# A two-layer block on one core: one rotation table, split modulation loads, paired squares, a shorter 1/rms and a divided FFN buffer

## The chip, the cores and the metric

The kernel runs on one core of one Trainium2 chip. The metric is the device time of one execution in microseconds (us). The core has five engines that run their own instruction streams and wait for each other through semaphores: TensorE (PE, matmul, with its weight loads PEld), VectorE (DVE), ScalarE (ACT), GpSimd (POOL) and SyncE (SP), which here issues the weight loads.

## The reference

Two transformer layers stand one behind the other, on 512 tokens of 1024 features, all in float32. What is computed, in short:

```python
# first layer
sh1, sc1, gt1, sh2, sc2, gt2 = adaln_params(c, w_mod, b_mod)     # silu(c) @ w_mod + b_mod
px = project(modulate(x, norm1_g, sh1, sc1), w_in)               # the same for ctx, 256 tokens
og = gla_bidir(...)                                              # gated linear attention, two directions
od = diff_attend(rope(rms(q)), rope(rms(k)) with ctx keys, v)    # differential attention
x = x + gt1 * (concat(merge(og), merge(od)) @ w_out)
x = x + gt2 * swiglu(modulate(x, norm2_g, sh2, sc2), w_ffn_in, w_ffn_out)
# second layer
h = rms_norm(x, mix_pre_g) @ w_in                                # pooling, forgetting attention, gates
x = x + rms_norm(mix, mix_post_g)
x = x + rms_norm(mem_attention(rms_norm(x), rms_norm(mem)))      # 256 memory tokens
x = x + rms_norm(conv_ffn(rms_norm(x), w_up, conv_w, w_down))    # hidden width 2816
```

Every norm divides by a root of a mean square over the 1024 features (or over a head). The modulation vectors come from a product of a 2-row matrix (c and c_ctx) with 1024 x 6144 weights.

## The kernel before, in words

**Layout and precision.** Activations stand feature-major, as eight tiles of 128 features by 512 tokens. A float32 product is made of three fast products: each operand is split in a high and a low part (`hi`, `lo`), and hi.hi, lo.hi and hi.lo are summed in PSUM. `wsplit` (L171) loads a weight piece of 512 KB to a ring buffer `wf` (two buffers), casts it on ACT to `whi` (L185), and subtracts on DVE or POOL to `wlo` (L186). `mm3` (L194 to L196) issues the three matmuls. So each weight piece costs one load, one ACT cast, one DVE subtraction and its matmuls.

**Start.** `normed_x` (L424) squares the eight tiles of x, by turns on ACT and DVE, and `sum_sq` (L308) sums each over features by four small matmuls with a vector of ones. `warm` (L483) issues spare transposes of an identity: 12 ahead of the first sum, two ahead of each later one (WU, WX). `rms` (L150 to L169) turns the sum into r = 1/rms by a logarithm and an exponential on ACT and a correction step on DVE; `bcast` (L326) spreads r over partitions by matmuls against the identity (L329), and ACT copies it out (L330). The first modulation tiles (`mod_tiles`, L350) come by 1 MB loads; ACT copies the sum (`mr`), two transposes (L362) bring it to columns, and DVE reduces it (L363).

**The first layer's middle.** Sixteen units of the linear attention (chunk, head) run in order from about 190 to 310 us. Projections, modulation steps and later work are "fillers": a list of closures with a length each, of which `fill_in` runs as many as fit between two parts of a unit. A modulation step (`mod_step`, L750 to L768) loads 512 KB of `w_mod` to the same ring `wf` as the weights and issues four matmuls (L762) into a PSUM bank; after four steps ACT copies 128 x 512 out (L766), and `mod_end` transposes it by four matmuls (L362). Twenty-four steps stand in units 0 to 11, two in each; eight stand in the filler list between `mem_in` and `mem_k`. The table of rotations is loaded once to `cs64`; GpSimd multiplies it by the key gain into `csk` and by the query gain in place (L630 to L635).

**Second norm of the first layer.** The output projection gives x in two halves of 256 tokens; `norm2` (L1299) computes sums (L311), r_n and its broadcast for each half, with pauses (`yield`) in which other matmuls are issued; W4 says how many stand ahead of the sums.

**FFN.** `ffn_hidden` (L1330) keeps the hidden activations as `Fhi` and `Flo`, and while these are empty uses parts of them as room for split weights (L1339, L1340). The second layer's FFN opens its pool `fp2` when the last residual update, `X<-X,KV` (L1428), is still running; the pool lies where `KV` and `Ym`, the halves of the branch just added, lay.

**Order.** The kernel names instructions behind which others are issued (`issue_after`, `queued`), and each engine executes its own list strictly in the order of the built program. SP's list holds nearly all loads, so a load that waits for its buffer holds back all loads behind it.

## Time and profile before

| | us |
|---|---|
| median of three runs | 1653.22 |
| lowest, highest | 1652.99, 1656.14 |
| the profiled execution's own time | 1654.39 |
| its span in the trace | 1652.6 |
| PE busy | 1600.5 (97%) |
| PE weight loads busy | 1359.2 (82%) |
| DVE busy | 948.7 (57%) |
| ACT busy | 716.8 (43%) |
| POOL busy | 214.1 (13%) |

The page lists the busy time of each engine over the whole span; the views quoted below list single instructions in order of time, who waited for whom, and the busy time of engines in short stretches with the clock that TensorE was granted (1.00 is 2.4 GHz, 0.50 is 1.2 GHz). In a row of a timeline the bracket at the end is the time for which the engine stood idle ahead of the instruction and who released it.

### The profile page before, as it was taken

The numbers are of one execution on the slowest core, as the hardware profiler recorded it, in microseconds if no ns is written. First come the engines' busy times: TensorE is split into PE (matmuls) and PEld (weight loads), VectorE is DVE, ScalarE is ACT, GpSimd is POOL, SyncE is SP. The second block draws the span as 40 slices with busy tenths as digits, with TensorE's granted clock in tenths as the row PEclk, the third lists the DMA queues.
The fourth block names the chain that finished last, engine by engine and source line by source line (L and its number), as shares of the span: only waits on it lengthen the run. The fifth ranks groups of instructions, "written<-read, shape, count | busy, mean of one in ns | idle before, by whom it ended". The sixth has DMA issues, their size and how long they took to land.

```text
span 1652.6 us, 25497 instructions
## 1 busy us (share of the span) xinstructions
PE 1600.5 (97%) x10146; PEld 1359.2 (82%) x10146; DVE 948.7 (57%) x1799; ACT 716.8 (43%) x1345; POOL 214.1 (13%) x236
## 2 busy tenths in 40 slices
PE   8998999999999999999999999999998999999997
PEld 6898877768999888888889777888988988888887
DVE  5647787868756222223335676445788777776333
ACT  3534445567745323232223565224466544444221
POOL 0400000111012222110004000122000222221001
PEclk9999999999999999999999999999999999999998
DMA  9132245232323333332332212234210223323332
GB/s 373 53 95 81 79 152 160 80 122 74 130 72 109 90 91 101 102 91 89 101 117 71 77 39 64 90 102 146 86 50 27 90 90 102 102 90 96 96 93 74
DMA packets 48903, 162.98 MB, mean 99 GB/s; under 512 B 5648, under 2 KB 11280, under 8 KB 47248
## 3 DMA queue, kind: packets, MB, share of 16 engines
q1 hardware_dynamic: 45040, 157.74, 30.5%
q10 hardware_dynamic: 3456, 3.33, 0.7%
q8 instruction: 80, 1.31, 0.3%
q0 software_dynamic: 288, 0.28, 0.1%
q14 instruction: 39, 0.32, 0.1%
HBM read 158.46 MB, written 3.15 MB: 98 GB/s over the span
## 4 chain that ended last, share of the span: by engine, by line
PE 87%; DVE 6%; ACT 3%; issue 2%; DMA 1%; POOL 1%; ACTq 0%; DVEq 0%; POOLq 0%
PE acc L194 16%; PE acc L195 16%; PE acc L196 16%; PE s L195 5%; PE s L196 5%; PE s L194 5%; PE acc L284 3%; PE acc L283 2%; PE acc L285 2%; PE mis L1135 2%; PE mis L1607 1%; PE acc L762 1%; DVE wlo L186 1%; DMA wm<-in_w_mod 1%; PE s L1106 1%
## 5 line engine op out<-in xcount | busy, mean ns | idle before, releaser
L185 ACT CAST whi<-wf 128x1024 fp32r<-128x1024 f32 (+4 forms) x221 | 228.7, 1035 | 421.1 <-PE acc L195 291.0
L186 DVE TENSOR_TENSOR wlo<-wf,whi 128x1024 fp32r<-128x1024 f32 (+2 forms) x183 | 221.7, 1211 | 176.2 <-ACT whi L185 170.8
L195 PE MATMUL acc<-qlo,whi 128*128 128x512 f32 (+1 forms) x640 | 238.9, 373 | 0.0
L196 PE MATMUL acc<-qhi,wlo 128*128 128x512 f32 (+1 forms) x640 | 238.9, 374 | 0.0
L194 PE MATMUL acc<-qhi,whi 128*128 128x512 f32 (+1 forms) x640 | 238.6, 373 | 0.0
L194 PEld LDWEIGHTS acc<-qhi,whi 128*128 128x128 f32 x640 | 120.7, 189 | 19.7
L195 PEld LDWEIGHTS acc<-qlo,whi 128*128 128x128 f32 x640 | 120.6, 189 | 19.6 <-issue 0.2
L196 PEld LDWEIGHTS acc<-qhi,wlo 128*128 128x128 f32 x640 | 120.7, 189 | 19.4
L195 PE MATMUL s<-qlo,whi 128*128 128x512 f32 (+1 forms) x336 | 127.4, 379 | 0.0
L194 PE MATMUL s<-qhi,whi 128*128 128x512 f32 (+1 forms) x336 | 127.4, 379 | 0.0
L196 PE MATMUL s<-qhi,wlo 128*128 128x512 f32 (+1 forms) x336 | 127.4, 379 | 0.0
L186 POOL TENSOR_TENSOR wlo<-wf,whi 128x1024 fp32r<-128x1024 f32 x38 | 90.9, 2393 | 213.5 <-ACT whi L185 213.5
L1392 DVE TENSOR_TENSOR e<-e,s 128x512 f32<-128x512 f32 (+1 forms) x22 | 14.3, 652 | 154.0 <-PE s L196 153.8
L195 PE MATMUL acc<-glo,whi 128*128 128x512 f32 (+1 forms) x208 | 74.5, 358 | 0.1
L196 PE MATMUL acc<-ghi,wlo 128*128 128x512 f32 (+1 forms) x208 | 74.2, 357 | 0.0
L194 PE MATMUL acc<-ghi,whi 128*128 128x512 f32 (+1 forms) x208 | 74.2, 357 | 0.0
L194 PEld LDWEIGHTS s<-qhi,whi 128*128 128x128 f32 x336 | 63.2, 188 | 11.9
L196 PEld LDWEIGHTS s<-qhi,wlo 128*128 128x128 f32 x336 | 63.2, 188 | 11.9
L195 PEld LDWEIGHTS s<-qlo,whi 128*128 128x128 f32 x336 | 63.2, 188 | 11.6
L194 PE MATMUL acc<-Fhi,whi 128*128 128x512 f32 (+1 forms) x187 | 71.5, 383 | 0.0
L196 PE MATMUL acc<-Fhi,wlo 128*128 128x512 f32 (+1 forms) x187 | 71.5, 383 | 0.0
L195 PE MATMUL acc<-Flo,whi 128*128 128x512 f32 (+1 forms) x187 | 71.5, 382 | 0.0
(648 smaller groups left out, 3832.0 us busy)
## 6 DMA issues: line engine op xcount, KB each, us to landing
wf<-in_w_ffn_in SPq DMA_DIRECT2D x44, 512.0 KB, 3.6
wf<-in_w_up SPq DMA_DIRECT2D x44, 512.0 KB, 3.5
wm<-in_w_mod SPq DMA_DIRECT2D x32, 512.0 KB, 4.1
wm<-in_w_mod SPq DMA_DIRECT2D x8, 1024.0 KB, 13.1
wf<-in_w_ffn_out SPq DMA_DIRECT2D x16, 512.0 KB, 3.6
wf<-in_w_g SPq DMA_DIRECT2D x16, 512.0 KB, 3.5
wf<-in_w_down SPq DMA_DIRECT2D x16, 512.0 KB, 3.5
wf<-in_w_dv SPq DMA_DIRECT2D x8, 512.0 KB, 4.2
```

Of the source, the lines that this page charges most:

```text
L185: A.copy(hi[:, :n], wf[:, :n])
L186: (lo_eng or V).tensor_tensor(lo[:, :n], wf[:, :n], f32(hi[:, :n]), ALU.subtract)
L194: T.matmul(o, lhi, rhi, start=start, stop=False)
L195: T.matmul(o, lhi, rlo, start=False, stop=False)
L196: ins = T.matmul(o, llo, rhi, start=False, stop=stop).ins
L283: T.matmul(o, bhi(k), whi, start=k == 0, stop=False)
L284: T.matmul(o, bhi(k), wlo, start=False, stop=False)
L285: T.matmul(o, blo(k), whi, start=False, stop=k == KT - 1)
L762: T.matmul(p[32 * j:32 * j + 32, 256 * h:256 * h + 256], silc[:, 4 * kc + j], wf[:, j * 256:(j + 1) * 256], start=kc == 0, stop=kc == 1, s ...
L1106: T.matmul(s_[:, n0:n1], QF[:, c, ts], KA[:, c, n0:n1], start=True, stop=False)
L1135: T.matmul(p[:, :128], aT[:, kt * 128:(kt + 1) * 128], v, start=kt == 0, stop=kt == NKT - 1)
L1607: T.matmul(pO[:, ts], vz[:, kt, hp_, 64 * e:64 * e + 128], pT[:, kt * 128:(kt + 1) * 128], start=kt + e == 0, stop=kt - t + e == 1, skip_g ...
```

## The change

Eight edits, none of which alters what is computed:

1. Start: squares in pairs. ACT squares tile k, DVE squares tile k+1 and adds the two; `sum_sq` runs four times instead of eight. The DVE square has one buffer. WU goes from 12 to 15, WX from 2 to 1. The first modulation tiles are queued behind the last sum, and the broadcast of r is cut in two around the transposes. The load of `cols` goes from ACT's queue to SP's.
2. `rms`: the logarithm reads the sum in PSUM with scale and bias, DVE forms v beside it, and three DVE operations follow where there were four.
3. The first loads of `memT` on ACT's queue are issued behind a later instruction (`hi_at`).
4. One rotation table: `csk` goes; `cs64` is turned for the keys, loaded again behind the w_dv loads, and turned for the queries (`turn_q`).
5. Modulation: of each two steps the first loads to a buffer of its own, the second to the ring; a group is two steps and 256 columns instead of four and 512, so ACT copies and `mod_end` come after every unit. The eight late steps go in groups of two behind two gate jobs and the first two `mem_k` jobs, and `mem_k` comes directly behind `mem_in`.
6. Second norm: the residual updates of the three finished parts come ahead of their squares; W4 goes from 2 to 1, and for the second half three pauses instead of one stand between sums and broadcast.
7. `ffn_hidden`: `Fhi` is cut in `Fhi` (7 tiles) and `Fend` (4 tiles, allocated first), rooms are taken from tiles 0 to 5 in order, and `zl` is allocated at its first use.
8. The ring's buffer count gets a name (NWF, 2 as before).

```diff
-WU, WX, WW = 12, 2, 5
+WU, WX, WW = 15, 1, 5
-W4, W5 = 2, 1
+W4, W5 = 1, 1
...
+        A.activation(y, src, AF.Ln, scale=scale, bias=epsc)
         V.tensor_scalar(v, src, scale, EPS, ALU.mult, ALU.add)
-        A.activation(y, v, AF.Ln)
         last_rs[0] = A.activation(y, y, AF.Exp, scale=-0.5).ins
-        V.tensor_tensor(t, y, y, ALU.mult)
-        V.tensor_tensor(t, t, v, ALU.mult)
-        V.tensor_scalar(t, t, -0.5, 1.5, ALU.mult, ALU.add)
-        V.tensor_tensor(r, y, t, ALU.mult)
+        V.scalar_tensor_tensor(t, v, -0.5, y, ALU.mult, ALU.mult)
+        V.tensor_tensor(t, t, y, ALU.mult)
+        V.scalar_tensor_tensor(r, t, 1.5, y, ALU.add, ALU.mult)
...
-        nc.scalar.dma_start(cols, a["cols"])
+        nc.sync.dma_start(cols, a["cols"])
...
-            for k in range(KT):
-                t = st2.tile([128, S], F32, tag=f"sqt{k % 2}", name="sqt")
-                if k % 2:
-                    V.tensor_tensor(t, x[:, k], x[:, k], ALU.mult)
-                else:
-                    A.activation(t, x[:, k], AF.Square)
+            for k in range(0, KT, 2):
+                t, u = (st2.tile([128, S], F32, tag=f"sqt{j}", name="sqt", bufs=2 - j) for j in range(2))
+                A.activation(t, x[:, k], AF.Square)
+                V.tensor_tensor(u, x[:, k + 1], x[:, k + 1], ALU.mult)
+                V.tensor_tensor(u, u, t, ALU.add)
                 with tc.issue_after(warm(WU if k == 0 else WX)):
-                    sum_sq(pt, t, k == 0, k == KT - 1)
+                    last_warm[0] = sum_sq(pt, u, k == 0, k == KT - 2)
...
-        mod_tiles(8)
-        next(nx)
-        im = mod_tiles(0)
+        queued(last_warm[0], lambda: mod_tiles(8))
+        ins = next(nx)
+        im = queued(ins, lambda: mod_tiles(0))
+        with tc.issue_after(ins):
+            next(nx)
...
+    def turn_q():
+        nc.sync.dma_start(cs64, a["rope"])
+        turn("q_g")
+    turn("k_g")
...
+        if (w, hf) == ("w_dv", 0) and len(fillers) == 12:
+            fillers.append((0.0, turn_q))
...
-        nc.scalar.dma_start(m, a["memT"][:, k])
+        with tc.issue_after(hi_at[0]):
+            nc.scalar.dma_start(m, a["memT"][:, k])
...
-        wf = ring.tile([128, RW], F32, tag="wf", name="wm", bufs=2)[:, :1024]
+        wf = ring.tile([128, RW], F32, tag="wf", name="wm", bufs=NWF)[:, :1024] if kc else \
+            mid2.tile([128, 1024], F32, tag="wm", name="wm", bufs=1)
...
-        if h == 1 and kc == 1:
-            mr = mid2.tile([128, 512], F32, tag="mr", name="mr")
-            A.copy(mr, p)
+        if kc == 1:
+            mr = mid2.tile([128, 256], F32, tag="mr", name="mr")
+            A.copy(mr, p[:, :256])
...
-        if u % 2 == 0:
-            mod_end()
+        mod_end()
...
+    mods_left = [[(0.8, mod_step), (0.8, mod_step), (0.3, mod_end)] for _ in range(MU, 16)]
     for m in range(GR, 4):
         fillers.append(gr_jobs[m])
+        fillers += mods_here()
...
-    for n in range(MU // 2, 8):
-        fillers += [(0.8, mod_step) for _ in range(4)] + [(0.6, mod_end)]
     for m in range(4):
         fillers.append((1.45, lambda m=m: mem_k(m)))
+        fillers += mods_here()
...
         r = fm_stats(sp, sqs[:, x:y], "n2")
-        yield
+        for _ in range(3 if x else 1):
+            yield
         bcast(rb[:, x:y], r)
...
-            ev_out(m, 0, S, p)
+            V.scalar_tensor_tensor(X[m], p, mods[:, 16 + m, 0:1], X[m], ALU.mult, ALU.add)
+        for m in range(len(parts)):
+            add_sq(X[m], m, 0, S)
...
-        early = fp.tile([128, NP, 2, S // 2], F32, tag="Fh2", name="early")
+        NT = FT - KT - NP
+        last = fp.tile([128, 4, S], F32R, name="Fend")
         rest = []
         for n in ("Fhi", "Flo"):
-            t = fp.tile([128, FT - KT - NP, S], F32R, name=n)
+            t = fp.tile([128, NT if rest else NT - 4, S], F32R, name=n)
             rest.append(t)
-        room = [t[:, 2 * j:2 * j + 2].rearrange("p k s -> p (k s)") for t in rest for j in range(5)]
-        room = [None] * 3 + [(room[j], room[5 + j], None) for j in (2, 3, 4, 0, 1)]
+        F[0] += [last[:, k] for k in range(4)]
+        early = fp.tile([128, NP, 2, S // 2], F32, tag="Fh2", name="early")
+        room = [t[:, 2 * j:2 * j + 2].rearrange("p k s -> p (k s)") for t in rest for j in range(3)]
+        room = [None] * 3 + [(room[j], room[3 + j], None) for j in range(3)]
```

TensorE at the program's start, before: the rows are spare transposes (`s<-ident`), sums of squares (`mis<-ones,sqt`), modulation matmuls (`acc<-wm,silc`) and the broadcast of `r_x`.

```order
L485 MATMUL s_128<-ident 128x128 x12
L311 MATMUL mis<-ones,sqt 128x32 x4
L485 MATMUL s_128<-ident 128x128 x2
L311 MATMUL mis<-ones,sqt 128x32 x4
...
L350 MATMUL acc<-wm,silc 32x256 x8
L329 MATMUL mis<-ident,r_x 128x128 x4
L362 MATMUL acc<-ident,mr 128x128 x2
L350 MATMUL acc<-wm,silc 32x256 x8
L485 MATMUL s_128<-ident 128x128 x3
```

The sum and its two transposes alternate eight times there. The same place after:

```order
L488 MATMUL s_130<-ident 128x128 x15
L313 MATMUL mis<-ones,sqt 128x32 x4
L488 MATMUL s_130<-ident 128x128
L313 MATMUL mis<-ones,sqt 128x32 x4
...
L353 MATMUL acc<-wm,silc 32x256 x8
L332 MATMUL mis<-ident,r_x 128x128 x2
L365 MATMUL acc<-ident,mr 128x128 x2
L332 MATMUL mis<-ident,r_x 128x128 x2
L353 MATMUL acc<-wm,silc 32x256 x8
L488 MATMUL s_130<-ident 128x128 x3
```

Here they alternate four times, with one transpose between two sums, and each sum waits for two DVE operations.

SP's loads in the first layer's middle, before: `wf` are weight pieces, `wm` modulation pieces, all in the one ring.

```order
L176 DMA wf<-in_w_dv 128x1024 x4
L176 DMA wf<-in_w_dq 128x1024 x4
L757 DMA wm<-in_w_mod 128x1024 x10
L176 DMA wf<-in_w_dv 128x1024 x2
L757 DMA wm<-in_w_mod 128x1024 x10
L176 DMA wf<-in_w_dv 128x1024 x2
L757 DMA wm<-in_w_mod 128x1024 x4
L176 DMA wf<-in_w_gr 128x1024 x4
L176 DMA wf<-in_w_xk 128x1024
L757 DMA wm<-in_w_mod 128x1024 x8
```

After, every second `wm` has a buffer of its own:

```order
L178 DMA wf<-in_w_dv 128x1024 x4
L642 DMA cs_99<-in_rope 128x512
L178 DMA wf<-in_w_dq 128x1024 x4
L770 DMA wm<-in_w_mod 128x1024 x7
L178 DMA wf<-in_w_dv 128x1024 x2
L770 DMA wm<-in_w_mod 128x1024 x8
L178 DMA wf<-in_w_dv 128x1024
L770 DMA wm<-in_w_mod 128x1024
L178 DMA wf<-in_w_dv 128x1024
L770 DMA wm<-in_w_mod 128x1024 x7
```

The second load of the rotation table stands ahead of the w_dq loads, one modulation load has gone ahead to the w_gv loads, and the w_dv loads stand fewer modulation steps behind.

ACT where the second FFN begins, before, with the semaphores that each row waits for: `sqx` is a square of x for the norm, `qhi` the high part of the normed x, `Fhi<-wf` the first split of a weight into the empty FFN buffer.

```order
L1430 ACTIVATE qhi<-X_5327,cols 128x256 [waits DVE_49]
L1430 ACTIVATE qhi<-X_5327,cols 128x256
L1432 ACTIVATE sqx<-X_5327 128x512 [waits DVE_49]
L185 CAST Fhi<-wf 128x1024 [waits DMAHW6_49,DVE_49]
L1767 ACTIVATE early<-z,cols 128x256 [waits DVE_49] x2
```

After:

```order
L1455 ACTIVATE qhi<-X_5343,cols 128x256 [waits DVE_49]
L1455 ACTIVATE qhi<-X_5343,cols 128x256
L1457 ACTIVATE sqx<-X_5343 128x512 [waits DVE_49]
L187 CAST Fhi<-wf 128x1024 [waits DMAHW7_49,DVE_49]
L1794 ACTIVATE early<-z,cols 128x256 [waits DVE_49] x2
```

The order is the same and the cast waits for DVE in both; the DVE instruction that releases it is in both programs the last `X<-X,KV`.

DVE at the same place, before:

```order
L1427 TENSOR_TENSOR KV<-KV,rbp 128x512
L1436 SCALAR_TENSOR_TENSOR qlo<-X_5327,cols,qhi 128x256 [waits Activation_49]
L1428 TENSOR_TENSOR X_5327<-X_5327,KV 128x2x256 [waits DVE_49]
L1436 SCALAR_TENSOR_TENSOR qlo<-X_5327,cols,qhi 128x256 [waits Activation_49]
L1763 TENSOR_TENSOR z<-acc,rb 128x256 [waits DVE_49]
L1763 TENSOR_TENSOR z<-s_12326,rb 128x256
L186 TENSOR_TENSOR Flo<-wf,Fhi 128x1024 [waits DMAHW6_49,Activation_49]
```

After:

```order
L1452 TENSOR_TENSOR KV<-KV,rbp 128x512
L1461 SCALAR_TENSOR_TENSOR qlo<-X_5343,cols,qhi 128x256 [waits Activation_49]
L1453 TENSOR_TENSOR X_5343<-X_5343,KV 128x2x256 [waits DVE_49]
L1461 SCALAR_TENSOR_TENSOR qlo<-X_5343,cols,qhi 128x256 [waits Activation_49]
L1790 TENSOR_TENSOR z<-acc,rb 128x256 [waits DVE_49]
L1790 TENSOR_TENSOR z<-s_12333,rb 128x256
L188 TENSOR_TENSOR Flo<-wf,Fhi 128x1024 [waits DMAHW7_49,Activation_49]
```

Nothing has moved in these seven rows.

## Rows read from the trace of the kernel before

**Rows 1.** The page, part 1: busy us, share of the span, instructions of each engine

```profile
PE 1600.5 (97%) x10146; PEld 1359.2 (82%) x10146; DVE 948.7 (57%) x1799; ACT 716.8 (43%) x1345; POOL 214.1 (13%) x236
```

**Rows 2.** Timeline of PE, 1.5 to 27 us: start, length, instructions, idle before

```profile
1.85 4.65 PE L485 MATMUL s<-ident 128*128 128x128 f32 x24 [1.85 <-POOL down L556]
6.34 0.98 PE L311 MATMUL mis<-ones,sqt 128*128 128x32 f32 x8
7.15 0.69 PE L485 MATMUL s<-ident 128*128 128x128 f32 x4
...
16.63 1.07 PE L350 MATMUL acc<-wm,silc 128*32 128x256 f32 x16
```

**Rows 3.** Timeline of all engines, 16.5 to 26 us

```profile
17.80 0.17 DVE L167 TENSOR_SCALAR t_x<-t_x 128x4 f32<-128x4 f32 x1
18.00 0.16 DVE L168 TENSOR_TENSOR r_x<-y_x,t_x 128x4 f32<-128x4 f32 x1
...
24.07 0.69 DVE L380 TENSOR_TENSOR hlo<-mx,hhi 128x512 fp32r<-128x512 f32 x1
```

**Rows 4.** Stretches: us, busy PE, PEld, DVE, ACT, POOL, granted clock, DMA share, GB/s

```profile
7.00:12.00 5.00, 5.00 (x47) 5.00 (x46) 2.21 (x5) 1.89 (x3) 0.00 (x0) 1.00 1.01 405
196.00:200.00 4.00, 1.93 (x40) 1.00 (x38) 3.95 (x9) 0.39 (x2) 0.00 (x0) 1.00 0.60 211
200.00:202.00 2.00, 2.00 (x16) 1.30 (x12) 1.81 (x5) 0.33 (x2) 0.00 (x0) 0.50 0.00 0
```

**Rows 5.** What PE waited for, 190 to 400 us: total us, times, longest

```profile
PE acc L762 <- DMA wm<-in_w_mod: 4.4, 4, 1.8
...
PE acc L283 <- ACT whi L185: 1.3, 1, 1.3
...
PE acc L284 <- DVE wlo L186: 0.9, 1, 0.9
...
PE acc L283 <- ACT mr L766: 0.7, 1, 0.7
PE s L362 <- DVE t_og L167: 0.6, 1, 0.6
```

**Rows 6.** Stretch of 20 us in the linear attention, columns as in rows 4

```profile
190.00:210.00 20.00, 17.21 (x235) 12.04 (x234) 17.83 (x46) 8.15 (x24) 0.00 (x0) 0.91 0.44 132
```

**Rows 7.** The page, part 6: loads, KB each, median us to landing

```profile
wm<-in_w_mod SPq DMA_DIRECT2D x32, 512.0 KB, 4.1
```

**Rows 8.** Line 653, uses of the rotation table: ns, first and last start in us

```profile
L653 DVE TENSOR_TENSOR kdv<-acc,csk x8: 414/415/417, 113.5 to 147.7; 128x256 f32<-128x256 f32 x8
L653 DVE TENSOR_TENSOR dq__1933<-acc,cs x8: 409/414/417, 180.3 to 229.1; 128x256 f32<-128x256 f32 x8
```

**Rows 9.** What PE waited for, 440 to 520 us

```profile
PE acc L194 <- DVE X L1297: 1.5, 1, 1.5
PE mis L329 <- DVE r_n L168: 1.3, 1, 1.3
PE mis L311 <- DVE sqs L1293: 0.3, 1, 0.3
```

**Rows 10.** Stretch in the second norm, columns as in rows 4

```profile
500.00:502.00 2.00, 1.66 (x14) 1.48 (x14) 0.57 (x3) 0.84 (x2) 0.00 (x0) 1.00 0.67 201
```

**Rows 11.** Timeline of all engines where the second FFN begins

```profile
1276.97 0.68 DVE L1428 TENSOR_TENSOR X<-X,KV 128x512 f32<-128x512 f32 x1
...
1277.68 1.05 ACT L185 CAST Fhi<-wf 128x1024 fp32r<-128x1024 f32 x1 [0.97 <-DVE X L1428]
...
1278.76 1.23 DVE L186 TENSOR_TENSOR Flo<-wf,Fhi 128x1024 fp32r<-128x1024 f32 x1
...
1278.78 0.58 PE L194 MATMUL s<-qhi,Fhi 128*128 128x256 f32 x1 [4.89 <-ACT Fhi L185]
```

**Rows 12.** What PE waited for, 1290 us to the end

```profile
PE mis L1800 <- DVE r_post L168: 1.6, 1, 1.6
PE mis L329 <- DVE r_pre L168: 0.8, 1, 0.8
```

More of the change, by code (lines that the diff above doesn't have):

```diff
@@ L31 @@
 FA, FG, FC, A0, GR, MU = 3.4, 2.5, 5.6, 2, 2, 12
-PJ, FP = 19, 8
+PJ, FP = 20, 8
 NF = 2
+NWF = 2
 T0 = 1
@@ L119 @@
     mods = const.tile([128, 48, 2], F32, name="mods")
+    epsc = const.tile([128, 1], F32, name="epsc")
     nc.gpsimd.memset(ones, 1.0)
+    nc.gpsimd.memset(epsc, EPS)
     make_identity(nc, ident)
@@ L173, in wsplit @@
         if wf is None:
-            wf = ring.tile([128, RW], F32, tag="wf", name="wf", bufs=2)
+            wf = ring.tile([128, RW], F32, tag="wf", name="wf", bufs=NWF)
         if shape is None:
@@ L310, in sum_sq @@
         for t in range(sq.shape[-1] // 128):
-            T.matmul(pt[:, 32 * t:32 * t + 32], sq[:, t * 128:(t + 1) * 128], ones, start=start and t == 0, stop=stop,
-                     skip_group_check=True)
+            ins = T.matmul(pt[:, 32 * t:32 * t + 32], sq[:, t * 128:(t + 1) * 128], ones, start=start and t == 0, stop=stop,
+                           skip_group_check=True).ins
+        return ins
     def fm_stats(pool, sq, name):
@@ L351, in mod_block @@
                            start=k < 4, stop=k >= 4, skip_group_check=True, tile_position=(0, 32 * j)).ins
-        mr = mpool.tile([128, 128 * n], F32, tag="mr", name="mr")
+        mr = mpool.tile([128, 128 * n], F32, tag="mr", name="mr", bufs=1)
         mr_at[0] = A.copy(mr, p).ins
@@ L626, with turn @@
     nlam = lam[:, 3:4]
-    turn = {"k_g": midp.tile([128, 2, TT, 64], F32, name="csk"), "q_g": cs64}
-    for n, cs in turn.items():
+    def turn(n):
         g = r_(n).rearrange("p (o d) -> p o d", o=1).to_broadcast([128, TT, 64])
         gs = r_(n).rearrange("p (o y f) -> p o y f", o=1, y=2)[:, :, ::-1].to_broadcast([128, TT, 2, 32])
-        G.tensor_tensor(cs[:, 0], cs64[:, 0], g, ALU.mult)
-        G.tensor_tensor(cs[:, 1].rearrange("p t (y f) -> p t y f", y=2),
-                        cs64[:, 1].rearrange("p t (y f) -> p t y f", y=2), gs, ALU.mult)
+        G.tensor_tensor(cs64[:, 0], cs64[:, 0], g, ALU.mult)
+        s4 = cs64[:, 1].rearrange("p t (y f) -> p t y f", y=2)
+        G.tensor_tensor(s4, s4, gs, ALU.mult)
+    def turn_q():
+        nc.sync.dma_start(cs64, a["rope"])
+        turn("q_g")
+    turn("k_g")
     sums_of = {}
@@ L812 @@
     Rq = gp.tile([128, NLEV, 128], BF16, name="Rq")
-    lt0 = ring.tile([128, RW], F32, tag="wf", name="lt0", bufs=2)
+    lt0 = ring.tile([128, RW], F32, tag="wf", name="lt0", bufs=NWF)
     nc.sync.dma_start(lt0[:, :NLEV * 128], a["LT"])
     V.tensor_copy(LT, lt0[:, :NLEV * 128])
-    lt1 = ring.tile([128, RW], F32, tag="wf", name="lt1", bufs=2)
+    lt1 = ring.tile([128, RW], F32, tag="wf", name="lt1", bufs=NWF)
     nc.sync.dma_start(lt1[:, :512], a["Lsm"])
@@ L1750 @@
     with tc.tile_pool(name="fp2", bufs=1) as fp:
-        zl = fp.tile([128, 2, 4, 2], F32, name="zl")
+        zl = []
         def pair2(pg_, pu_, i, x, y, held):
             ready(rb_of, x)
+            if not zl:
+                zl.append(fp.tile([128, 2, 4, 2], F32, name="zl"))
             res = []
```

31 lines of the change are left out of this document (18 added, 13 removed).

## The prediction

> **What bounds the kernel now.** I read the page's busy times first: PE is busy 1600.5 us of a 1652.6 us span [rows 1]. Nothing in the change takes work off PE but some small sums at the start, so what it can win lies in the 52 us in which PE stands idle and in the stretches in which its granted clock is at the lower level. Then I asked, stage by stage, what PE waits for. Four places bear on the change. At the start PE works through squares of x as they come [rows 2]. In the linear and differential attention it waits for modulation loads, for splits of weights and for copies out of PSUM [rows 5], while DVE is busy 17.83 of 20 us, so it is close to a second bound [rows 6]. The second norm of the first layer has three small waits [rows 9]. And the opening of the second FFN has the largest single one, 4.89 us [rows 11]. At the end two norms are waited for [rows 12]. Between these places PE runs full, and an edit to another engine costs or gains nothing there.
>
> The sum is made against the profiled execution, 1654.39 us; the median of the three runs, 1653.22, is 1.2 below it, and I carry that over.
>
> **Start.** The 24 matmuls of warming take 4.49 us, from 1.85 to 6.34 [rows 2]; 15 spare transposes instead of 12 make 30 of them, so the first sum starts at about 7.46. Four rounds follow instead of eight. In one round DVE squares and adds, two operations of 128x512 at 0.69 [rows 3], and PE sums for 0.81, from 6.34 to 7.15 [rows 2]. With one buffer for DVE's square these three follow one another: 2.19 us. Three rounds and a last sum end at 7.46 + 6.57 + 0.81 = 14.84, where the old ones end at 16.63 [rows 2]: 1.8 earlier, and with the shorter 1/rms (below) 2.2. But in a round PE is then busy 0.81 and one transpose (two matmuls, half of the 0.69 in rows 2), about 1.15 of 2.19. The trace shows what such a share did elsewhere: with PE busy 1.93 of 4.00 us the granted clock was 0.50, 1.2 GHz, in the 2 us behind it, whereas it was 1.00 while PE was busy 5.00 of 5.00 at the start [rows 4]. If it falls here, two of the sums take 1.62 and the 1.07 us block of modulation matmuls [rows 2] takes 2.14: 1.6 + 1.1 = 2.7 lost, which is more than was won; the broadcast behind them may lose as much as that block again. Ends -2.2 and +1.6; I take -0.4, nearer to the fall, because the row with the half busy share is the nearer one.
>
> The Trainium skill ("TensorE: Matmul & The Clock Gate", section "HAM oscillation — how this bites in real kernels") ties a fall of the clock to one long idle gap between bursts of matmuls; the gaps of the new rounds, about 1 us each, would not count, and the start would keep its 2.2. The trace speaks against it: no wait of PE in rows 5 is longer than 1.8 us, and the clock fell all the same.
>
> **1/rms.** The logarithm no longer waits for v, and one DVE operation of the chain goes. An operation there takes 0.16 and the next starts 0.20 later [rows 3]: 0.36 for each chain that PE waits for. The two behind 1290 us are waited for 0.8 and 1.6 [rows 12], so they give 0.36 each: -0.7. The chains ahead of the second FFN and r_n are in their own terms, r_x is in the start; elsewhere PE has other matmuls meanwhile.
>
> **Modulation loads.** Half of the 32 loads get a buffer of their own, which is free one whole step earlier, and the other half share the ring with weights in half the number. The four waits for `wm`, 4.4 us, should go [rows 5]; a load lands 4.1 us after its issue [rows 7], and a step now has a whole unit's time. Of the waits for `whi` and `wlo` behind the w_dv loads, 1.3 + 0.9, I take half, since those loads stand behind fewer steps: -1.1. The stretch at 200 us where the clock was 0.50 [rows 4] should shorten: 2 us at half speed, -1.0. Against that stand 16 ends (copy on ACT, two transposes, reduction on DVE) for 8. Eight ends cost PE 0.7 for the copy and 0.6 for a PSUM buffer [rows 5]; in proportion, 8 more cost at most +1.3, and since a copy is now made every unit I take +1.7. Sum -4.4 - 1.1 - 1.0 + 1.7 = -4.8. The lower end, -7.6, has all waits gone and free ends. The upper end is 0 or above, and is a rival.
>
> **Rotation table.** The second load waits until the keys are turned, whose last use starts at 147.7; the queries use the table first at 180.3 [rows 8]. In the 32 us between stand one load, half the size of one that takes 4.1 [rows 7], and two GpSimd operations. It is queued on SP ahead of the w_dq loads, which would be held back if the keys were late; then the cost is at most a load, 4.1. I take 0: the DVE work that it waits for is done first in the built order too. `memT` and `cols` move on queues whose loads nobody waits for at these places: 0.
>
> **Second norm.** The wait for X, 1.5, comes from a weight split that stands ahead of the update on DVE [rows 9], and the built order of DVE there is unchanged, so it stays. The wait for r_n, 1.3, goes: r_n now stands ahead of a weight split where it stood behind it. But the sums come 24 matmuls behind the last product instead of 36, and at 1.66 us for 14 [rows 10] PE is there 1.4 us earlier for squares that are no earlier: the 0.3 wait for `sqs` grows by that. Sum 0; ends -2.8 (X goes too, the squares follow) and +1.4.
>
> **FFN buffer.** The new first tile takes `KV`'s place and `Fhi` stands clear of it, so the cast should not have to wait for the last `X<-X,KV`. In the built program it does wait for it, and the rows on ACT and DVE have not moved. That update starts at 1276.97, the cast at 1277.68, the `lo` split at 1278.76, PE at 1278.78 [rows 11]. So the 4.89 stay but for the two shorter 1/rms chains ahead: -0.4. Were the wait gone, the cast could start when ACT is free, 0.97 earlier by its own idle time [rows 11], but `Flo` still stands behind the same DVE work: at best -1.4.
>
> **Sum.** -0.4 - 0.7 - 4.8 + 0 + 0 - 0.4 = -6.3: 1648.1 for a profiled execution, 1646.9 for the median; I say 1647.
>
> **Rivals.**
> - The clock holds at the start, as the skill's rule would have it: 1.8 better, 1645. Against it stands the half busy share; for it that the new rounds are regular and start from full speed. 0.12.
> - All load waits go and the ends are free: -7.6 instead of -4.8, and 0.5 of the second norm: 1643.5. For it: the buffers are there. Against it: DVE at 17.83 of 20 [rows 6]. 0.15.
> - What PE no longer waits for a load it waits for DVE: the chain of a unit runs over DVE at 89%, and the whole -4.8 is given back: 1651.5. For it: rows 6, and eight more reductions on DVE. Against it: the waits for loads in rows 5 are ends of chains that DVE had nothing to do with. 0.22.
> - Slower: the ends. Each of the 16 now stands inside a single unit, between its scores and its output, and takes a PSUM buffer of the kind that the unit needs next. If an end costs PE 0.9 us instead of the 0.16 (1.3 over 8) seen, it is 16 x 0.9 = 14.4 where the sum holds 1.3 + 1.7: +11.4, 1658. It decides from about 0.8 each; the worst seen, copy and buffer together, is 0.7 + 0.6 = 1.3 [rows 5]. Against it: most of the eight showed no wait. 0.11.
> - The FFN buffer does what it says: inside the range, -1.0 more; the built order speaks against it, and it changes no case.
>
> **How the numbers follow.** The forecast has 0.40. About 0.2%, 3.3 us, is what a measurement of this kernel can tell from no change: faster is under 1649.9, slower over 1656.5. Of the forecast 0.33 lies under 1649.9 and 0.07 within; of the first rival 0.11 and 0.01; the second is faster; of the third 0.02 is faster, 0.18 the same and 0.02 slower; the fourth is slower but for 0.01. Faster 0.61, same 0.27, slower 0.12. The range runs from 1640.5, where the clock holds, the loads' waits go and the second norm gains, to 1655, where the load term is given back and the start and the second norm stand at their upper ends; a tenth lies beyond either end.
>
> **What the profile after would show.** The four waits for `wm` gone from rows 5, and the 20 us at 190 with PE over 18; a sum round of about 2.2 us, the clock in the stretch behind 12 us, the modulation block ahead of 16.6 or not; r_n without a wait and `sqs` with one over 1 us; the 4.89 at the second FFN still over 4. It would be wrong most plainly if new waits for `mr` or PSUM buffers follow each unit, if the stall at the second FFN is gone, or if the clock stays low far beyond the start.

## The result, and the profile after

The changed kernel takes 1641.05 us (median of four runs, 1640.55 to 1642.52) where the kernel before took 1653.11 beside it: a ratio of 0.9926, with a 95% interval of 0.9909 to 0.9943. That is 12 us faster. The forecast was 1647 and 6.3 us faster, so the sign is right and the time lies just inside the range, at its lower edge, but half of the gain has no term in the sum. The experiments show that this is no small slip: most of the gain comes from a part of the change that the sum never priced, and one term that it did price has the wrong sign.

The profiled execution after takes 1641.52 us, with a span of 1639.1. The first row of the page after, as in [rows 1] (busy us, share, instructions):

```profile
PE 1590.6 (97%) x10098; PEld 1355.6 (83%) x10098; DVE 948.0 (58%) x1791; ACT 718.7 (44%) x1353; POOL 214.1 (13%) x237
```

PE is busy 9.9 us less. It has 48 matmuls fewer, all at the start: 32 of the sums and 16 of the spare ones, some 6 us by [rows 2]. What it lost by half clock is the same in sum as before, 13 us, but lies elsewhere, as will be seen.

**The start became longer, not shorter.** PE's timeline of the kernel after (start, length, idle before and what ended it), to compare with [rows 2]:

```profile
7.17 0.98 PE L313 MATMUL mis<-ones,sqt 128*128 128x32 f32 x8
...
11.05 1.08 PE L313 MATMUL mis<-ones,sqt 128*128 128x32 f32 x8 [2.60 <-DVE sqt L434]
...
13.71 1.92 PE L313 MATMUL mis<-ones,sqt 128*128 128x32 f32 x8 [1.28 <-DVE sqt L434]
...
17.20 1.92 PE L313 MATMUL mis<-ones,sqt 128*128 128x32 f32 x8 [1.00 <-DVE sqt L434]
19.05 1.94 PE L353 MATMUL acc<-wm,silc 128*32 128x256 f32 x16
...
26.60 0.51 PE L196 MATMUL s<-hhi,whi 128*128 128x512 f32 x1 [0.86 <-ACT hhi L381]
```

The modulation block that began at 16.63 begins at 19.05 and takes 1.94 where it took 1.07. The sums double from 0.98 to 1.92. The stretches of the kernel after show why (columns as in [rows 4]; the last but two is the granted clock):

```profile
8.00:10.00 2.00, 0.45 (x4) 0.26 (x3) 0.60 (x2) 0.36 (x1) 0.00 (x0) 1.00 1.07 434
10.00:12.00 2.00, 0.95 (x9) 0.95 (x9) 0.89 (x2) 0.63 (x1) 0.00 (x0) 1.00 0.98 414
12.00:14.00 2.00, 0.72 (x6) 0.53 (x5) 1.39 (x2) 0.00 (x0) 0.00 (x0) 0.65 0.97 395
14.00:16.00 2.00, 2.00 (x10) 1.91 (x9) 0.34 (x1) 0.00 (x0) 0.00 (x0) 0.50 1.05 373
20.00:22.00 2.00, 2.00 (x17) 1.19 (x10) 0.32 (x2) 0.37 (x1) 0.00 (x0) 0.50 1.03 434
24.00:26.00 2.00, 1.73 (x16) 1.41 (x12) 1.80 (x5) 1.59 (x3) 0.00 (x0) 1.00 1.03 426
```

From 14 to 22 us the engine is at 1.2 GHz (0.50), and at 24 us it is back at 2.4.

**The linear attention is fuller.** The stretch of [rows 6] and that of the clock in [rows 4], in the kernel after, and between them the stretch that lies about the first product of the linear attention as [rows 6] does (that product starts at 208.1 us here and at 199.6 before):

```profile
190.00:210.00 20.00, 19.73 (x212) 17.39 (x214) 18.75 (x50) 10.61 (x22) 0.00 (x0) 1.00 0.24 80
...
198.50:218.50 20.00, 19.56 (x267) 15.57 (x266) 19.26 (x56) 10.37 (x29) 0.00 (x0) 1.00 0.31 106
...
200.00:202.00 2.00, 2.00 (x18) 1.95 (x17) 1.85 (x7) 0.42 (x2) 0.00 (x0) 1.00 0.05 8
```

PE is busy 19.56 of 20 us where it was 17.21, at full clock where the mean was 0.91. The 19.73 between the same two times are mostly work ahead of the units. What PE waited for from 185 to 400 us, after (total us, times, longest), beside [rows 5]:

```profile
PE s L1118 <- ACT p L1124: 1.5, 2, 1.1
PE mis L1020 <- DVE AT L1012: 1.2, 2, 1.0
PE acc L285 <- ACT whi L187: 0.9, 1, 0.9
...
PE acc L775 <- DMA wm<-in_w_mod: 0.2, 1, 0.2
```

The 4.4 us for `wm` are 0.2. What stands on top now are a chain through ACT in the differential attention, 1.5, and one through DVE inside a unit of the linear attention, 1.2.

**The second norm and the second FFN.** The waits of PE from 400 to 530 us, after, beside [rows 9]; then the opening of the second FFN, all engines, beside [rows 11]:

```profile
PE mis L313 <- DVE sqs L1312: 2.2, 1, 2.2
PE acc L196 <- DVE X L1343: 1.9, 1, 1.9
```

```profile
1265.01 0.69 DVE L1453 TENSOR_TENSOR X<-X,KV 128x512 f32<-128x512 f32 x1
...
1265.74 1.04 ACT L187 CAST Fhi<-wf 128x1024 fp32r<-128x1024 f32 x1 [0.97 <-DVE X L1453]
...
1266.82 1.23 DVE L188 TENSOR_TENSOR Flo<-wf,Fhi 128x1024 fp32r<-128x1024 f32 x1
...
1266.84 0.58 PE L196 MATMUL s<-qhi,Fhi 128*128 128x256 f32 x1 [4.50 <-ACT Fhi L187]
```

The wait for `r_n` is gone and the one for the squares went from 0.3 to 2.2. At the FFN the same chain ends the same wait: the cast begins when the last update of X is done, with 0.97 of idle time on ACT before it, as in the kernel before.

### The profile page after: what moved, and what is told of

It reads as the page before. It is cut to its first block, busy times and chain, and to the rows that moved or that the text cites. A ratio compares the mean times of both kernels' runs of the same rounds, so it can differ in the third digit from the quotient of the medians.

```text
span 1639.1 us, 25459 instructions
## 1 busy us (share of the span) xinstructions
PE 1590.6 (97%) x10098; PEld 1355.6 (83%) x10098; DVE 948.0 (58%) x1791; ACT 718.7 (44%) x1353; POOL 214.1 (13%) x237
## 4 chain that ended last, share of the span: by engine, by line
PE 85%; DVE 5%; ACT 3%; DMA 1%; issue 1%; POOL 0%; ACTq 0%; DVEq 0%; POOLq 0%
PE acc L197 16%; PE acc L198 16%; PE acc L196 16%; PE s L198 5%; PE s L196 5%; PE s L197 5%; PE acc L286 3%; PE acc L285 3%; PE acc L287 3%; PE mis L1147 1%; PE mis L1632 1%; DVE wlo L188 1%; PE acc L775 1%; PE s L1118 1%; DMA mk<-in_memT 1%
## 5 line engine op out<-in xcount | busy, mean ns | idle before, releaser
L285 PE MATMUL acc<-whi,hhi 128*128 128x256 f32 (+1 forms) x224 | 67.1, 299 | 3.4 <-ACT qsq L654 2.5
L286 PE MATMUL acc<-wlo,hhi 128*128 128x256 f32 (+1 forms) x224 | 65.6, 293 | 3.3 <-DVE wlo L188 3.3
## 6 DMA issues: line engine op xcount, KB each, us to landing
wm<-in_w_mod SPq DMA_DIRECT2D x8, 1024.0 KB, 11.7
```

The costliest lines, as they stand in the source:

```text
L285: T.matmul(o, bhi(k), whi, start=k == 0, stop=False)
L286: T.matmul(o, bhi(k), wlo, start=False, stop=False)
```

## The experiments

All times are compared with the kernel before on the same chip, so the ratios can be set against each other. Beside the time, five landmarks of each profiled execution tell where it was gained, since each landmark is the start of an instruction that all these kernels have: the first product of the normed x (`hhi`), the first product of `QX` with `E` in the linear attention (`QX`), the first product of the pooling branch (`mix`), the first product of the transposed scores in the attention over the memory (`xpT`), and the span. Each landmark comes from one execution.

| kernel | median us | ratio, 95% interval | hhi | QX | mix | xpT | span |
|---|---|---|---|---|---|---|---|
| before | 1653 to 1656 | 1 | 23.0 | 199.6 | 1020.8 | 1206.3 | 1652.6 |
| after | 1641.05 | 0.9926 [0.9909, 0.9943] | 26.6 | 208.1 | 1011.0 | 1194.6 | 1639.1 |
| e1 after, start as before | 1638.26 | 0.9894 [0.9876, 0.9912] | 23.9 | 202.9 | 1009.1 | 1192.7 | 1638.4 |
| e2 after, `cols` load as before | 1642.39 | 0.9917 [0.9901, 0.9934] | 27.1 | 206.8 | 1012.3 | 1195.5 | 1640.5 |
| e3 after, modulation as before | 1647.23 | 0.9957 [0.9940, 0.9973] | 28.1 | 207.8 | 1016.0 | 1199.7 | 1644.9 |
| e4 after, 1/rms as before | 1646.60 | 0.9945 [0.9930, 0.9960] | 28.0 | 201.9 | 1008.8 | 1195.0 | 1641.6 |
| e5 before, PJ 20 | 1640.74 | 0.9906 [0.9887, 0.9925] | 24.2 | 198.1 | 1009.1 | 1194.7 | 1639.1 |
| e6 after, PJ 19 | 1651.53 | 0.9977 [0.9964, 0.9989] | 28.6 | 211.1 | 1023.6 | 1206.9 | 1652.1 |
| e7 after, second norm as before | 1641.15 | 0.9915 [0.9897, 0.9932] | 29.2 | 207.8 | 1010.4 | 1194.0 | 1638.8 |
| e8 after, FFN buffer as before | 1642.95 | 0.9923 [0.9907, 0.9938] | 26.5 | 207.7 | 1013.7 | 1197.2 | 1642.5 |
| e9 before, PJ 20 and modulation | 1636.83 | 0.9888 [0.9873, 0.9903] | 24.1 | 197.3 | 1004.2 | 1189.8 | 1636.2 |
| e10 before, PJ 21 | 1639.36 | 0.9898 [0.9882, 0.9915] | 24.2 | 199.2 | 1008.9 | 1194.5 | 1639.2 |
| e11 before, PJ 20 and 1/rms | 1642.65 | 0.9918 [0.9902, 0.9935] | 22.9 | 201.9 | 1011.1 | 1194.4 | 1639.4 |
| e12 e2, five spare transposes | 1638.83 | 0.9907 [0.9889, 0.9925] | 22.5 | 202.5 | 1007.6 | 1190.9 | 1636.7 |

How far a landmark can be trusted the table shows itself: five kernels with the same start (after, e3, e6, e7, e8) have `hhi` between 26.5 and 29.2, four with the old one (before, e5, e9, e10) between 23.0 and 24.2. And two landmarks are not the same point of the work in all kernels: ahead of `QX` the kernels with 20 have done one projection more than those with 19, and `xpT` comes some 13 matmuls earlier in the list with the new 1/rms.

### The start: e1, e2, e12

e1 takes the whole start back (two buffers for `mr`, squares one by one, 12 and 2 spare transposes, the old order of the queue); the core of its diff:

```diff
-WU, WX, WW = 15, 1, 5
+WU, WX, WW = 12, 2, 5
...
-            for k in range(0, KT, 2):
...
-                V.tensor_tensor(u, u, t, ALU.add)
+            for k in range(KT):
```

> The changed kernel with the whole start as before (eight sums, two spare transposes between them, cols on ACT's queue, the broadcast in one piece). Theory A, from the trace after: the new start puts the first hhi product at 26.60 us where it was 22.99, so undoing it gives 3.6 us or a little more (clock): 1636 to 1638. Theory B, the forecast's own term: the new start is worth -0.4, so undoing it gives 1641 to 1642.

It is faster than the new kernel: 0.9894 against 0.9926, 5.3 us by the ratios, whose intervals just touch, and 2.8 by the medians. The first product with `hhi` stands 2.7 us earlier and the linear attention 5.2 us earlier; by `mix` 1.9 of it is left. So the new start costs 2 to 5 us, where the sum had it win 0.4.

e2 asks whether the load of `cols`, which was moved behind the tiles of x, is the reason (in the new kernel a DVE operation waits 2.52 us for it):

```diff
-        nc.sync.dma_start(cols, a["cols"])
+        nc.scalar.dma_start(cols, a["cols"])
```

> The changed kernel with one line undone: cols is loaded on ACT's queue again. Theory A: DVE stood from 6.88 to 9.40 us for cols, which lands behind the x tiles on SP's queue, and the second sum came 2.6 us late for it; undone, the second sum starts near 9.7 instead of 11.05 and 1 to 3 us come back: 1638 to 1640. Theory B: the rounds of half busy share bring the clock down anyway and the load hides: 1641.

No: the wait goes and the second sum begins at 10.30 instead of 11.05, but the other sums still take 1.9 and `hhi` begins at 27.1. The time is that of the new kernel.

e12 then adds to e2 nothing but spare work, which keeps PE busy in the gaps of a round:

```diff
-WU, WX, WW = 15, 1, 5
+WU, WX, WW = 15, 5, 5
```

> The new kernel with the load of cols back on ScalarE's queue (as in e2) and one number more: five spare transposes between the sums of the start, not one; they write nothing that is used. With e2 the sums began at 7.75, 10.30, 13.76 and 17.25, the last three at half clock, and the first product with hhi stood at 27.15. Theory A, the half-busy rounds are what lowers the clock: with five transposes TensorE has work through the round, the granted clock stays at 1.00 up to 24 us, each sum takes 0.98, a round some 2.5, the last sum begins near 15.4, the first product with hhi at 23 to 24.5, and the kernel gains 2 to 4 on e2: ratio 0.989 to 0.991. Theory B, the clock falls for another reason (the loads, the short sums themselves): it is 0.50 behind 12 us again, the transposes make the rounds longer, the first product with hhi stands at 27 or later, ratio 0.992 to 0.994.

PE's timeline of e12, and a stretch of it:

```profile
12.71 1.08 PE L313 MATMUL mis<-ones,sqt 128*128 128x32 f32 x8 [0.39 <-DVE sqt L434]
13.62 1.36 PE L488 MATMUL s<-ident 128*128 128x128 f32 x10
15.37 1.08 PE L313 MATMUL mis<-ones,sqt 128*128 128x32 f32 x8 [0.39 <-DVE sqt L434]
16.38 1.07 PE L353 MATMUL acc<-wm,silc 128*32 128x256 f32 x16
...
22.50 0.51 PE L196 MATMUL s<-hhi,whi 128*128 128x512 f32 x1 [0.87 <-ACT hhi L381]
```

```profile
14.00:16.00 2.00, 1.61 (x15) 1.43 (x14) 1.21 (x2) 0.00 (x0) 0.00 (x0) 1.00 1.00 396
```

With 12 transposes more, the last two sums take 1.08, not 1.91, the clock is 1.00 in every stretch of 2 us up to 28, the modulation block takes 1.07 again, and the first product with `hhi` comes 4.65 us earlier than in e2 and half a microsecond earlier than in the kernel before. All seven traces with one spare transpose in a round (after, e2, e3, e4, e6, e7, e8) have the clock at 0.50 from 14 to 22 us. That settles it: what made the start long was above all the clock that the half-idle rounds lost, and it stretched the chain too, since DVE's square has one buffer and waits for a sum that takes twice as long (2.01 us ahead of the last square in the new kernel, 1.17 in e12). The span is 3.8 us shorter than that of e2; the intervals of the two ratios overlap, so the size of the gain at the end is less certain than the landmark.

### The number PJ: e5, e6, e10

The first hunk of the diff sets PJ from 19 to 20. The list of eight edits ahead of the prediction leaves it out, and so does the diff quoted there. Ahead of the first unit of the linear attention, `fill_to(len(fillers) - PJ)` runs the first PJ entries of the filler list. Nineteen are ten of the twelve projections of the differential attention's keys, with the squares of the memory and their sum between them; the twentieth is the eleventh key projection, 24 matmuls, whose rotation on DVE then lies ahead of the units too. e5 is the kernel before with that one number:

```diff
-PJ, FP = 19, 8
+PJ, FP = 20, 8
```

> The kernel before with one number changed: PJ, the count of fillers that are run ahead of the linear attention, 20 instead of 19. Theory A: this number, which the prediction left out, moves one 24-matmul projection job ahead of the first unit, and all later fillers one place forward, so that the memory layer's steps come under the attention's first head instead of its second; of the 16.5 us that stretch 185 to 450 us won, about 6 are the modulation edit's and most of the other 10 are this: 1643 to 1647. Theory B: the order alone is worth nothing: 1652 to 1655.

It gives 0.9906: 15.5 us by the ratio and 14.0 by the medians, more than the whole change and more than either theory had. e6 is the reverse, the new kernel with 19:

```diff
-PJ, FP = 20, 8
+PJ, FP = 19, 8
```

> The changed kernel with PJ back at 19, all else changed. Theory A: it loses 6 to 10 us of its 12: 1647 to 1651. Theory B: nothing: 1640 to 1643.

It loses 10.5 us on the new kernel by the medians, 8.4 by the ratios (0.9977 against 0.9926), and is hardly faster than the kernel before. So the number is worth 8 to 10 us in the new kernel and 14 to 15 in the old one. Where: at the first `QX` e6 is 3.0 us behind the new kernel, and at `mix` 12.6; before and e5 stand 1.5 and 11.7 apart. At `QX` the kernels with 20 have done 24 matmuls more, so the gap there is larger than it looks; at `mix` the work done is the same. Of e6's 12.6, 2.0 stood at `hhi` already, ahead of anything that the number moves. Some of it shows as named waits. Ahead of the units (100 to 185 us), the wait for the split of the carried state, `ghc`, of before, e6 and after, in this order:

```profile
PE s L856 <- DVE ghc L830: 1.9, 2, 1.7
```

```profile
PE s L869 <- DVE ghc L843: 2.2, 2, 2.0
```

```profile
PE s L869 <- DVE ghc L843: 0.2, 1, 0.2
```

And in the units (185 to 450 us) of e6:

```profile
PE s L990 <- DVE E L978: 3.6, 6, 0.9
PE mis L1020 <- DVE AT L1012: 2.7, 5, 1.0
```

In the new kernel the same two are 0.5 and 1.2. Added up over stretches of 2 us from 100 to 450, PE's idle time and the time that it lost by working at half clock (busy time times one minus the granted clock) are 21.2 and 8.0 us before, 17.8 and 3.3 in e5, 18.4 and 1.7 in e6 and 12.2 and 1.7 in the new kernel. So one pair differs by 3.4 of idle time and 4.7 of clock, the other by 6.2 of idle time alone. That accounts for 8.1 of the 11.7 us at `mix` and for 6.2 of the 12.6, of which another 2.6 lie between 450 us and `mix`; the rest was not located. The order of the built program moves with the number: of the products with `KA` (the scores of the differential attention, behind the units), 20 stand ahead of the first product with `mhi` before and 14 in e5, 24 in e6 and 12 in the new kernel, so the output projection starts earlier, between the later heads of that attention. That this order is what gives the time is argued, not shown.

Is 20 a lucky value, or does it take one job ahead to be enough? e10 sets 21 in the kernel before:

```diff
-PJ, FP = 19, 8
+PJ, FP = 21, 8
```

> The kernel before with one number more: PJ at 21, so that two projection jobs more than before stand ahead of the linear attention, not one. Theory A, room: each projection job that is done ahead takes rotations and splits off DVE in the units, where it is busy nine tenths, so 21 is as good as 20 or better: 1636 to 1642, with the wait for ghc still gone and no wait for E over 1 us. Theory B, a chance of the order: 20 happens to fit, and with 21 the waits come back elsewhere, 1645 to 1653.

0.9898: as good as 20, and no better within the intervals, with all twelve key projections ahead of the units. The wait for `ghc` is gone here as well, and the first `mhi` stands behind 12 products with `KA`. So it is no chance of one value; it is a step between 19 and 20, not a slope. Which of the moved pieces makes it was not taken apart.

### The modulation loads: e3, e9

e3 puts the modulation steps of before (shared buffers, ends every second unit, the last steps in one place) in the new kernel:

```diff
-        wf = ring.tile([128, RW], F32, tag="wf", name="wm", bufs=NWF)[:, :1024] if kc else \
-            mid2.tile([128, 1024], F32, tag="wm", name="wm", bufs=1)
...
+        wf = ring.tile([128, RW], F32, tag="wf", name="wm", bufs=2)[:, :1024]
...
-        mod_end()
+        if u % 2 == 0:
+            mod_end()
```

> The changed kernel with the modulation steps as before (all in the ring, groups of four, ends after every second unit, eight late steps ahead of mem_k). Theory A: between 185 and 450 us PE's idle time fell from 16.8 to 8.2 us and the time lost at the lower clock from 8.7 to none, all of it from this edit: 1653 to 1657. Theory B, the forecast's term of -4.8: 1646. Theory C: most of it comes from the rest (the k table, orders): 1643.

It costs 5.1 us by the ratios (0.9957 against 0.9926, the intervals just touch) and 5.8 by the spans, and the waits of [rows 5] for loads and splits are back, the one for `wm` at half its size, the one for `whi` at twice (185 to 400 us of e3):

```profile
PE acc L285 <- ACT whi L187: 2.6, 2, 1.9
PE acc L774 <- DMA wm<-in_w_mod: 2.3, 3, 0.9
```

e9 is the other side: the kernel before with PJ 20, the modulation edit and the rotation table loaded twice, which makes the room for it.

> The kernel before with two parts of the change only: the constant PJ at 20, and the modulation loads in 16 units with a buffer of their own (with the rotation table loaded twice, which makes the room). Start, 1/rms, second norm and the buffer of the second FFN as before. Theory A, the parts add: with PJ alone 1640.7 was measured, and taking the modulation edit out of the new kernel cost 5, so 1635 to 1637, with no wait of TensorE for wm left and the start as before. Theory B, the two overlap: with PJ at 20 the four waits for wm are 2.9 us where they were 4.4, and what they free goes to waits for E and AT of the units, so 1639.5 to 1642.

0.9888, or 3.0 us better than PJ alone, though the two intervals overlap, and the lowest median of all: 18.8 us faster than before and some 6 faster than the new kernel, with the loads, the table and PJ alone. In this order of the program the first `QX` stands at 197.3 and the waits for `wm` are 1.5, not gone. At `mix` and still at `xpT` it is 4.9 us ahead of e5, at the end 2.9. Of the 2.0 behind `xpT`, 1.5 are a stretch that e5 does not have: from 1198 to 1204 us the granted clock of e9 is 0.79, 0.50 and 0.86.

### 1/rms: e4, e11

e4 takes 1/rms, five operations that follow one another and one beside them, back to seven in a row:

```diff
-        A.activation(y, src, AF.Ln, scale=scale, bias=epsc)
+        A.activation(y, v, AF.Ln)
...
-        V.scalar_tensor_tensor(t, v, -0.5, y, ALU.mult, ALU.mult)
-        V.tensor_tensor(t, t, y, ALU.mult)
-        V.scalar_tensor_tensor(r, t, 1.5, y, ALU.add, ALU.mult)
+        V.tensor_tensor(t, y, y, ALU.mult)
+        V.tensor_tensor(t, t, v, ALU.mult)
+        V.tensor_scalar(t, t, -0.5, 1.5, ALU.mult, ALU.add)
+        V.tensor_tensor(r, y, t, ALU.mult)
```

> The changed kernel with 1/rms in its old seven operations. Theory A: the shorter chain made the scheduler put the cast of the second w_gv piece behind the eight hc activations (2.9 us wait at 70.38 and 1.6 us of half clock behind it); with the old chain the built order has it ahead of them again, so that wait goes and the chains cost about 0.36 each again: 1637 to 1640. Theory B: the wait has another cause and the old chains cost 1 to 2 us: 1642 to 1643.

By the medians that costs 5.5 us, by the ratios 3.1, and the two intervals overlap; both theories had it lower. e11 gives the same edit to the kernel before, with PJ 20:

> The kernel before with PJ at 20 and 1/rms in five operations, all else as before. Theory A, the shorter 1/rms is worth what its removal from the new kernel cost, 3 to 4 us, wherever it stands: 1636.5 to 1638, against 1640.7 with PJ alone. Theory B, it is worth only the operation that is gone on the chains that TensorE waits for, under 1 us, and its larger effect in the new kernel came from how the order fell out there: 1639.5 to 1641.5, with the wait for wlo near 70 us present as in the new kernel.

Here it wins nothing: 0.9918 against 0.9906 without it, nearer to theory B. The landmarks say what happens. From `mix` to the end of the span the kernels with the new form take 628.1 to 629.3 us (after, e1, e2, e3, e6, e7, e8, e11, e12) and those with the old one 630.0 to 632.8 (before, e4, e5, e9, e10), and PE's idle time there is 16.2 to 16.9 us against 18.3 to 18.9: 2.0 gained. It comes at `xpT` and behind it. What PE waited for most near `xpT` (1185 to 1260 us), before and after:

```profile
PE mis L1707 <- ACT qhi L1430: 1.9, 1, 1.9
```

```profile
PE mis L1732 <- DVE sm L1723: 1.5, 2, 1.1
```

From `mix` to `xpT` the new form looks 2.2 us faster as well (183.2 to 183.7 against 185.5 to 186.2), but that is no gain: PE stands idle there for 0.1 us in the kernel before and in the new one, and the traces have 972 or 973 matmuls with the new form where they have 985 or 986 with the old. But at `mix` e11 is 2.0 later than e5, and the new kernel 2.2 later than e4: as much was lost before. DVE's timeline near 61 us, of e5 and then of e11, shows where:

```profile
61.17 0.75 DVE L380 TENSOR_TENSOR hc<-mc,hc 128x256 fp32r<-128x256 f32 x2
61.84 1.28 DVE L186 TENSOR_TENSOR wlo<-wf,whi 128x1088 fp32r<-128x1088 f32 x1
63.50 0.43 DVE L380 TENSOR_TENSOR hc<-mc,hc 128x256 fp32r<-128x256 f32 x1 [0.38 <-POOL mc L379]
```

```profile
63.57 0.42 DVE L382 TENSOR_TENSOR hc<-mc,hc 128x256 fp32r<-128x256 f32 x1 [0.38 <-POOL mc L381]
64.38 0.43 DVE L382 TENSOR_TENSOR hc<-mc,hc 128x256 fp32r<-128x256 f32 x1 [0.38 <-POOL mc L381]
64.72 1.28 DVE L188 TENSOR_TENSOR wlo<-wf,whi 128x1088 fp32r<-128x1088 f32 x1
```

With the shorter chain the built order sets the split of a weight piece, `wlo`, behind the run of `hc` steps, which wait for POOL one by one, where it stood after the second. PE waits for it: 30 to 185 us of e11 has

```profile
PE acc L285 <- ACT qsq L647: 2.9, 1, 2.9
PE acc L286 <- DVE wlo L188: 2.8, 1, 2.8
```

where `wlo` was 0.3 and `qsq` 1.1 before. The new kernel has 2.9 and 2.5; e4 has 0.4 for `wlo`, and `qsq` is not among its larger waits. So the edit shortens the chains in the second half and pays for it near 70 and 140 us by an order that nobody asked for. That e4 still ends later than the new kernel comes from behind `mix`: it has the idle time of the old form again, 18.9 us where the new kernel has 16.4, and PE at a clock of 0.87, 0.50 and 0.78 from 1204 to 1210 us, some 1.6 us, where the new kernel keeps 1.00.

### Second norm and FFN buffer: e7, e8

e7 restores the order of the second norm (one pause ahead of the broadcast, updates and squares by turns):

```diff
-W4, W5 = 1, 1
+W4, W5 = 2, 1
...
-        for _ in range(3 if x else 1):
-            yield
+        yield
...
-            V.scalar_tensor_tensor(X[m], p, mods[:, 16 + m, 0:1], X[m], ALU.mult, ALU.add)
-        for m in range(len(parts)):
-            add_sq(X[m], m, 0, S)
+            ev_out(m, 0, S, p)
```

> The changed kernel with the second norm of the first layer as before (updates and squares by turns, W4 at 2, one pause). Theory A, from the trace after: the wait for sqs grew from 0.3 to 2.2 and the one for X from 1.5 to 1.9 while that for r_n went, idle and half-clock time in 450 to 530 us rose from 3.1 to 5.7; undone, 1 to 2.5 us come back: 1638 to 1640. Theory B, the forecast's term of 0: 1641.

The time doesn't move. The waits of PE from 400 to 530 us in e7:

```profile
PE acc L196 <- DVE X L1316: 1.8, 1, 1.8
PE mis L313 <- DVE sqs L1312: 0.7, 1, 0.7
PE mis L332 <- DVE r_n L170: 0.3, 1, 0.3
```

They sum to 2.8, those of the new kernel to 4.1, and from 450 to 530 us the new kernel loses 1.7 us more at half clock, where before and e7 lose none. The edit trades `r_n` for `sqs`, at a loss of 2.9 us in that stage of the trace, which the times don't show.

e8 restores one tile for the second FFN's buffer:

```diff
-        last = fp.tile([128, 4, S], F32R, name="Fend")
...
-            t = fp.tile([128, NT if rest else NT - 4, S], F32R, name=n)
+            t = fp.tile([128, FT - KT - NP, S], F32R, name=n)
```

> The changed kernel with the FFN buffer in one piece, rooms 2, 3, 4 as before. Theory A, the forecast: the cast still waits for the last X<-X,KV, the buffer edit is worth nothing: 1641, PE's wait at the second FFN between 4.4 and 4.9. Rival: the edit is worth 1 to 5 us somewhere: 1642 to 1646.

```profile
PE s L196 <- ACT Fhi L187: 4.5, 1, 4.5
```

The wait at the opening of the second FFN (1255 to 1300 us of e8) is 4.5 with the old buffer and 4.5 with the new. The edit does nothing there, and the times are the same within the intervals. The 0.4 against the kernel before comes from the shorter 1/rms: e4, with the new buffer and the old 1/rms, has 4.9. Why the cast still follows the last update of X, though the edit was made to keep its tile off `KV`, is open.

## Why the prediction was right, and where it was not

**The part that carried the gain is not in the sum.** PJ stands in the first hunk, and the prediction prices each other hunk but never names it. It is one number, it changes no operation, and it moves a job of 24 matmuls past the beginning of the linear attention; alone it gives 14 to 15 us. The sum could have asked what it does: the counts of `KA` ahead of `mhi` (20 and 12) were there to be read in the built order. Its bounds could have come from the idle and half-clock time of that stage, 29 us from 100 to 450. What the sum of -6.3 does describe is e6, all other edits together at PJ 19; they measure 0.9977 [0.9964, 0.9989], or -3.8 us (-1.7 to -6.0), so it was too good by 2.5. The forecast came within 6 us of the result because a missing gain of 8 to 15 was partly offset by a start that it had too good by 2 to 6. That the time lies inside the range is luck in good part.

**Start: -0.4, measured +2 to +5** (2.7 at `hhi`, 5.2 at `QX`, 1.9 at `mix`, 2.8 by the medians and 5.3 by the ratios of e1 and after). The mechanism was put right, the balance wrong. The sum weighed 2.2 won against 2.7 lost and took a value between. The 2.2 rested on three rounds of 2.19, or 6.57; they took 3.88, 2.66 and 3.49, or 10.0 (the starts of the four sums above; the 3.88 has DVE's wait for `cols` in it). Even at full clock a round takes 2.66 (e12, 12.71 to 15.37). And a sum at half clock delays DVE's next square, which has one buffer: that is the 3.49, which the sum left out. Two sums and the block at half speed were counted, and the broadcast in the upper end alone (1.23 for four matmuls, 0.71 in e12); the rounds were left at their length. The rival by which the clock holds did not come, but e12 shows its condition: fill the rounds, and `hhi` begins at 22.50.

The Trainium skill ("TensorE: Matmul & The Clock Gate", section "HAM oscillation — how this bites in real kernels") would have let the clock hold, since it ties the fall to one long gap. The rows disagree: no gap from 7 to 27 us is longer than 2.60, and the clock was 0.50 from 14 to 22 us; in e2 the longest gap there is 1.28, and the clock was 0.60 already from 10 to 12. The next section of that page of the Trainium skill, "A second HAM failure mode: psum-queue depth-cycling", tells of a kernel in which frequent short idle times made the clock swing; these rows agree with that one.

**Modulation loads: -4.8, measured -5.1 in the new kernel (e3) and -3.0 beside PJ alone (e9).** The steps held in the main: `wm` from 4.4 to 0.2 (of which PJ alone takes 1.5: 2.9 are left in e5), `whi` and `wlo` from 2.2 to 1.3 together (half was taken). The clock at 200 us went from 0.50 to 1.00, but not by this edit: e3, without it, has 1.00 there too. What e3 has and the new kernel has not is a fall further on, 0.63 and 0.52 from 233 to 237 us, some 1.5 us: the 1.0 of the sum was of the right size, at another place. The rival by which DVE gives all of it back fell, though at PJ 19 a part of it came: in e6 the waits for `E` and `AT` are 3.6 and 2.7, where the kernel before has 1.3 and 0.4. The one by which the 16 ends cost 14 us fell too, as no wait for `mr` is left among the larger ones.

**1/rms: -0.7, and nothing by e11, -3 by e4.** In the second half it was worth more than the term, 2.0 us of idle time from `mix` to the end with the FFN's 0.4 in it: the waits near `xpT`, 1.9 and 0.5 before and 1.5 after, were in no term. And "elsewhere PE has other matmuls meanwhile" failed: a shorter chain changes the built order, and near 70 and 140 us that costs about 2. Of the two chains at the end that the term named, the waits of PE from 1300 us on have

```profile
PE mis L1827 <- DVE r_post L170: 1.3, 1, 1.3
```

where [rows 12] had 1.6: 0.3, close to the 0.36 that was put. The other, `r_pre`, went from 0.8 to 0.7 only.

**Second norm: 0, FFN buffer: -0.4.** The waits moved for the reasons given: `r_n` went, X stayed, `sqs` grew (by 1.9, where 1.4 was the estimate), and the FFN's 4.89 became 4.50. In the trace the second norm came out above its upper end of +1.4: idle time and the time lost at half clock from 450 to 530 us are 3.1 before and 5.7 after, 1.7 of it clock; e7 shows no difference in the time. The rival by which the buffer does what it says fell with e8. **Rotation table: 0.** Nothing speaks against it: e9 has it and the lowest median. It was not taken apart by a run of its own.

## What to carry to other kernels

Price every constant in a diff, above all those that say how much work stands ahead of a stage: compare the built order of both kernels at that stage, and let its idle and half-clock time be the bound. An edit that gives PE less to do in a stretch that it waits through can cost more than it saves, and spare matmuls there (e12) can keep the clock up. Before a gain is read from two landmarks, count the work between them. The lowest time here was that of two edits and one number (e9, 1636.83); e12's start and the chains behind `mix` with the new 1/rms gained in places of their own, but were not run together with it.
